# Five buffers for arriving weights in the MLP, taken from the up products' scratch, with the normed rows split by group and the loads of their sums moved ahead

## The chip, the core and the metric

The kernel runs on one core of one Trainium2 chip. The core has TensorE (PE in the profile; its weight loads are PEld), VectorE (DVE), ScalarE (ACT), GpSimd (POOL) and SyncE (SP), and 16 DMA engines that serve DMAs issued by SP, ACT and POOL. Each engine works through its own instructions in order. The metric is the device time in microseconds of one execution; lower is better.

## The reference, cut to what matters

```python
def encoder_layer(x, ...):
    h = rms_norm(x, g_mix)
    proj = h @ w_in                      # q, k, v, u/v of the gate, two gates
    attn = attention_mixer(q, k, v)      # 3 dilated windows, combined
    sgu = spatial_gating(u, vs, w_s, b_s, g_sgu)
    merged = sigmoid(ga) * (attn @ w_branch_a) + sigmoid(gb) * (sgu @ w_branch_b)
    x = x + merged @ w_out
    h2 = rms_norm(x, g_mlp)
    x = x + square(relu(h2 @ w_up)) @ w_down
    return x                             # then rms_norm(x, g_final)
```

There are 1536 tokens (512 of one request and 1024 of another), the width is 1024 and the MLP's inner width 4096; everything is float32. The change concerns the end of the `w_out` product, where `h2` is made, and the MLP.

## The kernel before, in words

**Split products.** A float32 matrix product is made of three passes of PE: each operand is split into a rounded part `hi` (a cast on ACT, line L153) and a rest `lo = src - hi` (a subtraction on DVE, L154), and `hi*hi`, `hi*lo` and `lo*hi` are added in PSUM.

**Weights.** `weight` (L157 to L164) brings one block of 512 x 128 or 128 x 512 weights: SP issues the load into a buffer `raw` (L159, 256 KB), ACT casts it to `hi`, DVE makes `lo`. There are N_RAW = 3 buffers `raw` and N_SPLIT = 5 pairs `hi`/`lo`, each used in turn. A load into a `raw` buffer waits until the split of the weight that was in it is done; a cast waits until PE has used the pair that it will overwrite.

**The w_out stage** (from about 1680 us to 1770 us). Two halves of columns times twelve tiles of 128 tokens. In the second half, each tile's finished row is stored (`x1_scr`, L819), normed (`h2`), transposed on PE (L744), multiplied by the gain on DVE (`h2T`, L746) and stored by SP to `h2_scr`, two stores of 512 x 128 per tile (L749).

**The MLP** (from 1774.75 us). The tokens form two groups of 768 (g = 0, 1). `h2` of a group, `w_up`, the activations and `w_down` are each cut into 2 x 2 blocks, and a product of two such matrices is made of seven products of blocks (`p1, p2, q3` to `q7`) instead of eight, by sums and differences of blocks. For each group there are eight steps c; a step has two up products (`up_products`, j = 0, 1: seven forms of 12 matmuls 128 x 384, L928) and one down product (`down_products`: seven forms of 18 matmuls 128 x 512, L979). Every form takes one weight in an up product and two in a down product, so 28 in a step. Below, U is the pair of up products of a step and D its down product.

In an up product DVE and ACT make the four blocks of activations out of the seven accumulators: `v` (L936), `z` (L943), `a22` (L946), `a21` (L951), `a12` (L956), then squares of their positive parts (ACT, L915 and L916) and the split forms for the down product. `q3` accumulates onto the bank of `q5`, which `a22` reads, and so its matmuls wait for `a22`. All these small results live in `unit` buffers of 128 x 384, twelve in turn.

**The forms of h2.** Each group starts from 28 blocks `hf` (seven forms times four k). `p1, p2, q4` are blocks of `h2` in `h2_scr`; `q3, q5, q6, q7` are sums of such blocks, made once on DVE and kept in `form_scr`. For group 0 the sums are made during the last tiles of the w_out stage: `diff_steps` gives a list of steps for each k (`loads`, then four sums, each with its store), all on POOL's queue, in rooms of rows that are already stored; `SUMS_AT` says how many steps follow each tile. For group 1 the same steps go along with group 0's steps c = 1 to 4 on SP's queue, in `unit` buffers. `form_steps` loads a block into a `unit` (`raw_form`, POOL's queue, L1026) and splits it (ACT, DVE); a load is issued N_FORM = 7 blocks ahead of the split. Group 0's forms enter in the first up product, group 1's in the last step of group 0, in its second up product and its down product.

**Other work.** Group 0's results are kept in `row_scr` and finished in group 1's steps 1 to 6 (`stored_steps`: loads of a row and of the gain on POOL's queue at L1061 and L240, a norm, a store). In a down product POOL makes three additions per tile (L995, L996, L1006).

**What sets the order.** A scheduler puts each engine's instructions in order from the program as written; `side()` hangs one step of the lists above behind each form of an up product and each tile of a down product.

Of the kernel before, what the change touches and what calls it, by code (L numbers as in the profile page):

```python
# [10 lines left out]
F32 = mybir.dt.float32  # L11
# [7 lines left out]
P = 128  # L19
DM = 1024  # L20
KB = DM // P
NTOK = 1536
# [10 lines left out]
BIG = 1e30  # L33
ROW = 2 * 64 + 4
EDGE = 24
N_SPLIT, N_RAW = 5, 3
QT = 2
STEPS = 49 / 36
XSTEP = 4
# [5 lines left out]
GT = NTOK // 2  # L45
HT = GT // 2
SUM_ROWS = 8
EARLY = 2
N_FORM = 7
SUMS_AT = {6: 1, 7: 5, 8: 5, 9: 5, 10: 4}  # L50
DIFFS = ("q3", "q5", "q6", "q7")
UP_ORDER = ("p1", "q6", "q7", "p2", "q5", "q4", "q3")
# [56 lines left out]
def encoder_kernel(ctx: ExitStack, tc: tile.TileContext, a):  # L109
    nc = tc.nc  # L110
# [8 lines left out]
    dram = ctx.enter_context(tc.tile_pool(name="dram", bufs=1, space=DRAM))  # L119
# [3 lines left out]
    wp = ctx.enter_context(tc.tile_pool(name="w", bufs=1))  # L123
# [11 lines left out]
    gate_scr = [dram.tile([P, NTOK], F32, name=f"gate_scr{m}") for m in range(EARLY)]  # L135
    form_scr = [dram.tile([len(DIFFS), 4, P, HT], F32, name=f"form_scr{g}") for g in range(2)]
    row_scr = dram.tile([GT, DM], F32, name="row_scr")
    h2_scr = dram.tile([KB, P, NTOK], F32, name="h2_scr")
    x1_scr = dram.tile([NTOK, DM], F32, name="x1_scr")
    up_sums = {k: dram.tile([DM // 2, DFF // 2], F32, name=f"up_{k}") for k in SUMS}  # L140
    down_sums = {k: dram.tile([DFF // 2, DM // 2], F32, name=f"down_{k}") for k in SUMS}
# [10 lines left out]
    def split(hi, lo, src, eng=nc.vector):  # L152
        nc.scalar.copy(hi, src)  # L153
        eng.tensor_sub(lo, src, hi.bitcast(F32))  # L154

    def weight(src, k, pair=None, eng=nc.vector):

        raw = wp.tile([P, 512], F32, tag="raw", name="raw", bufs=N_RAW).rearrange("p (k n) -> p k n", k=k)
        nc.sync.dma_start(out=raw, in_=src.rearrange("(k p) n -> p k n", p=P))  # L159
        if pair is None:  # L160
            pair = (wp.tile([P, 512], F32R, tag=s, name=s, bufs=N_SPLIT) for s in ("hi", "lo"))
        hi, lo = (t.rearrange("p (k n) -> p k n", k=k) for t in pair)
        split(hi, lo, raw, eng)
        return hi, lo  # L164
# [10 lines left out]
    def product_steps(out, terms):  # L175
        n = len(terms)
        for i, ((sh, sl), (mh, ml)) in enumerate(terms):
            nc.tensor.matmul(out, sh, mh, start=i == 0, stop=False)  # L178
            nc.tensor.matmul(out, sh, ml, start=False, stop=False)  # L179
            nc.tensor.matmul(out, sl, mh, start=False, stop=i == n - 1)  # L180
            yield
# [75 lines left out]
    with ExitStack() as ph:  # L257
# [6 lines left out]
        def load_x(t):  # L264
            raw = vpool.tile([P, 1024], F32, tag="x", name="x", bufs=2)
            parts = row_parts()
            for i in range(2):
                cols = slice(i * 512, (i + 1) * 512)
                eng = (nc.scalar, nc.sync)[i] if t == 0 else nc.gpsimd
                eng.dma_start(out=raw[:, cols], in_=x_rows[t][:, cols])  # L270
                if t == 0 and i:
                    junk = vpool.tile([P, 512], F32, tag="junk", name="junk", bufs=1)
                    nc.vector.tensor_tensor_reduce(
                        out=junk, in0=raw[:, cols], in1=raw[:, cols], scale=0.5 / DM, scalar=0.0,
                        op0=ALU.mult, op1=ALU.add, accum_out=parts[:, i:i + 1])
                else:
                    square_sum(parts[:, i:i + 1], raw[:, cols], vpool)
            rstd = rstd_of(parts)
            for i in range(2):
                cols = slice(i * 512, (i + 1) * 512)  # L280
                normed(raw[:, cols], raw[:, cols], rstd, g_mix[:, cols])
            return raw
# [4 lines left out]
        with ExitStack() as ph_w:  # L287
# [8 lines left out]
            for ch in range(2):  # L296
# [6 lines left out]
                for t in range(NT):  # L303
                    more_x = ch == 0 and t + 1 < NT
                    if more_x:
                        raw = load_x(t + 1)
                    acc = acc_tile()
                    steps = product_steps(acc, token_terms(hT[t // 4], t, lambda k: tuple(x[:, 0, :] for x in w[k])))
# [62 lines left out]
    with ExitStack() as ph:  # L371
# [230 lines left out]
        for c in range(SUM_ROWS):  # L602
            n = DM // 2 // SUM_ROWS
            streams.append(block_sums(a["w_up"][0], up_sums, DM // 2, DFF // 2, c * n, n))
            n = DFF // 2 // SUM_ROWS
# [41 lines left out]
    with ExitStack() as ph:  # L647
# [3 lines left out]
        def half_tile(name):  # L651
            return fp.tile([P, 512], F32, tag="half", name=name)
# [34 lines left out]
        for n in range(NCH):  # L687
            sig = {}
            attT = tuple(resident2(f"att_{s}") for s in "hl")
            for i in range(2 * KB):  # L690
                s, m = divmod(i, KB)
# [14 lines left out]
            for k in range(KB):  # L706
                raw = half_tile("sgu_raw")
# [31 lines left out]
    def h_features(t, halves):  # L739

        for i, h in enumerate(halves):
            pt = tp_tile()
            for b in range(4):
                nc.tensor.transpose(pt[:, b * P:(b + 1) * P], h[:, b * P:(b + 1) * P], ident)  # L744
            hT2 = pp.tile([P, 512], F32, tag="half", name="h2T", bufs=2)
            nc.vector.tensor_mul(  # L746
                hT2.rearrange("p (k t) -> p k t", k=4), pt.rearrange("p (k t) -> p k t", k=4),
                g_mlp[:, 4 * i:4 * i + 4, None].to_broadcast([P, 4, P]))
            nc.sync.dma_start(  # L749
                out=h2_scr[4 * i:4 * i + 4, :, t * P:(t + 1) * P].rearrange("k p t -> p k t"),  # L750
                in_=hT2.rearrange("p (k t) -> p k t", k=4))

    def diff_steps(g, k, new, eng, wait):

        x = {}

        def load(key, r, s):
            x[key] = new()
            eng.dma_start(out=x[key], in_=h2_scr[4 * s + k, :, g * GT + r * HT:g * GT + (r + 1) * HT])

        def store(form, key):
            eng.dma_start(out=form_scr[g][DIFFS.index(form), k], in_=x[key])

        def loads():
            load("a", 0, 0)
            load("b", 1, 0)
            load("c", 1, 1)
            load("d", 0, 1)

        def first():  # L770
            nc.vector.tensor_sub(x["a"], x["a"], x["b"])
            store("q7", "a")

        def second():
            nc.vector.tensor_sub(x["b"], x["b"], x["c"])
            store("q5", "b")

        def third():
            nc.vector.tensor_add(x["c"], x["a"], x["c"])
            store("q6", "c")  # L780

        def fourth():
            nc.vector.tensor_sub(x["d"], x["d"], x["c"])
            store("q3", "d")

        return [loads] + [lambda: None] * wait + [first, second, third, fourth]

    sums = []
    for k in range(4):

        room = [x1[(2 * k + i // 2) % 6][:, i % 2 * HT:(i % 2 + 1) * HT] for i in range(4)]
        sums += diff_steps(0, k, lambda room=room: room.pop(0), nc.gpsimd, 0)
    for ch in range(2):
        cols = slice(ch * 512, (ch + 1) * 512)
        w = {}
# [1 line left out]
        for k in (range(KB), (6, 7, 0, 1, 2, 3, 4, 5))[ch]:  # L797
            pair = None
            if len(w) >= (0, 2)[ch] and len(w) < (6, 8)[ch]:
                if not spare:  # L800
                    r = resident2("w_out")
# [4 lines left out]
        for t in range(NT):  # L806
            acc = acc_tile()
            terms = token_terms(hT[t // 4], t, lambda k: tuple(x[:, 0, :] for x in w[k]))
            steps = product_steps(acc, [terms[k] for k in w])
# [30 lines left out]
    mp = ctx.enter_context(tc.tile_pool(name="mlp", bufs=1, reuse_waits="tile"))  # L840
    slabs = ctx.enter_context(tc.tile_pool(name="slabs", bufs=6, side="right", reuse_waits="tile"))
    ps3 = ctx.enter_context(tc.tile_pool(name="ps3", bufs=8, space=PSUM, reuse_waits="tile"))
    def unit(name):
        return mp.tile([P, HT], F32, tag="unit", name=name, bufs=12)

    def bank():
        return ps3.tile([P, 512], F32, tag="acc", name="acc")
# [47 lines left out]
            self(len(self.steps))  # L895

    side = Side()

    def slab_view(s):
        return s.rearrange("p a b c -> p (a b c)").bitcast(F32)[:, :DM]  # L900
# [110 lines left out]
    def form_source(g, form, k):  # L1011
        if form in DIFFS:
            return form_scr[g][DIFFS.index(form), k]
        r, s = {"p1": (0, 0), "p2": (0, 1), "q4": (1, 1)}[form]
        return h2_scr[4 * s + k, :, g * GT + r * HT:g * GT + (r + 1) * HT]

    def form_steps(g, fs):

# [3 lines left out]
        def step(i):  # L1022
            for j in range(i, min(i + N_FORM, len(items))):
                if j not in raws:
# [71 lines left out]
    x = None  # L1096
    CH = DFF // P // 4
    for g in range(2):
        for c in range(CH):
# [5 lines left out]
            for j in range(2):  # L1105
# [5 lines left out]
                if not c and j:  # L1111
                    x = {}
# [49 lines left out]
```

## Time and profile before

| | us |
|---|---|
| median of 3 runs (lowest, highest) | 2806.36 (2803.49, 2807.26) |
| profiled execution, its own time | 2803.75 |
| its span | 2802.0 |
| PE busy | 2692.5 (96%) |
| DVE busy | 1747.7 (62%) |
| ACT busy | 1290.1 (46%) |
| POOL busy | 422.5 (15%) |
| granted TensorE clock, mean | 0.986 |

A table by stretches gives for each stretch `A:B` (us from the span's start) its length, the busy time of each engine with its instructions in brackets, the granted clock as a share of full speed, the mean busy share of the DMA engines and GB/s. A row of the waits reads: engine and line that waits, `<-` who ended the wait, then us in total, times, longest. A row of the timeline begins with its start and its length in us; in square brackets stands the idle time before it and who ended it. A row of the DMAs gives KB each and the us from issue to landing.

### The profile page before, as it was taken

Reading aid. Unit: us, or ns where it says so; the run is one execution under the profiler, and the core shown is the slowest. Engines: PE = TensorE matmul, PEld = TensorE weight load, DVE = VectorE, ACT = ScalarE, POOL = GpSimd, SP = SyncE. Lnnn points to the kernel's source line nnn. Section 1 sums busy time; section 2 is a strip of 40 time slices with the busy share of each in tenths; the row PEclk is TensorE's granted clock in tenths of the full one; section 3 lists DMA queues with packets and bytes.
Section 4 is the critical chain, followed back from the end, with each engine's and each line's share of the span. In section 5 each row is a group of like instructions: output and inputs, shape, how many; then the busy total and the mean of one; then the engine's idle time right before and its main releaser. Section 6 shows DMA issues by size and latency. Waiting matters only on the chain.

```text
span 2802.0 us, 38921 instructions
## 1 busy us (share of the span) xinstructions
PE 2692.5 (96%) x13400; PEld 2309.0 (82%) x13400; DVE 1747.7 (62%) x3722; ACT 1290.1 (46%) x2766; POOL 422.5 (15%) x507
## 2 busy tenths in 40 slices
PE   7999999999999999999999999899999989999997
PEld 5788888888888887888888887788989878888886
DVE  5542200166666666556555526788888868888888
ACT  5421111255556566553434321555556545555555
POOL 1000000011121212100000002222211322222222
PEclk9999999999999999999999999899999989999998
DMA  3112222247576768554443437654544555444443
GB/s 128 53 49 75 89 76 79 87 112 179 151 176 180 174 174 193 132 153 140 136 144 119 141 118 244 229 150 146 152 143 129 161 189 156 141 142 136 139 143 128
DMA packets 376439, 391.16 MB, mean 140 GB/s; under 512 B 23088, under 2 KB 290352, under 8 KB 372656
## 3 DMA queue, kind: packets, MB, share of 16 engines
q1 hardware_dynamic: 337008, 253.85, 30.3%
q0 software_dynamic: 28112, 86.83, 12.8%
q10 hardware_dynamic: 11120, 47.98, 5.0%
q8 instruction: 106, 1.74, 0.3%
q14 instruction: 93, 0.76, 0.1%
HBM read 333.22 MB, written 122.45 MB: 163 GB/s over the span
## 4 chain that ended last, share of the span: by engine, by line
PE 35%; DVE 8%; DMA 6%; issue 4%; ACT 4%; POOL 3%; DVEq 0%; SPq 0%; ACTq 0%; POOLq 0%
PE acc L979 7%; PE acc L178 7%; PE acc L180 7%; PE acc L179 7%; PE acc L928 6%; DVE lo L154 3%; DMA raw<-up_q 3%; ACT hi L153 1%; POOL x L996 1%; POOL x L995 1%; DVE act L154 1%; DMA raw<-in_w_down_dram 1%; ACT a L916 1%; ACT a L915 1%; ACT act L153 1%
## 5 line engine op out<-in xcount | busy, mean ns | idle before, releaser
L154 DVE TENSOR_TENSOR lo<-raw,hi 128x512 fp32r<-128x512 f32 x695 | 556.2, 805 | 420.8 <-ACT hi L153 413.8
L153 ACT CAST hi<-raw 128x512 fp32r<-128x512 f32 x696 | 430.6, 619 | 686.4 <-PE acc L179 238.3
L178 PE MATMUL acc<-res_h,hi 128*128 128x512 f32 x1344 | 556.2, 414 | 0.8 <-DVE stg L579 0.8
L180 PE MATMUL acc<-res_h,lo 128*128 128x512 f32 x1344 | 526.5, 392 | 0.0
L179 PE MATMUL acc<-res_l,hi 128*128 128x512 f32 x1344 | 525.3, 391 | 0.0
L928 PE MATMUL acc<-hf,hi 128*128 128x384 f32 x1792 | 471.6, 344 | 46.0 <-DVE a L946 24.8
L979 PE MATMUL acc<-hi,act 128*128 128x512 f32 x1344 | 423.9, 395 | 6.6 <-ACT hi L153 6.6
L928 PEld LDWEIGHTS acc<-hf,hi 128*128 128x128 f32 x1792 | 331.8, 193 | 59.2 <-ACT hi L153 30.8
L979 PEld LDWEIGHTS acc<-hi,act 128*128 128x128 f32 x1344 | 255.6, 191 | 61.4 <-ACT hi L153 8.9
L928 PE MATMUL acc<-hf,lo 128*128 128x384 f32 x896 | 306.1, 342 | 0.0
L180 PEld LDWEIGHTS acc<-res_h,lo 128*128 128x128 f32 x1344 | 252.4, 188 | 54.5
L179 PEld LDWEIGHTS acc<-res_l,hi 128*128 128x128 f32 x1344 | 254.3, 189 | 36.0
L178 PEld LDWEIGHTS acc<-res_h,hi 128*128 128x128 f32 x1344 | 254.0, 189 | 36.4 <-DVE stg L579 0.9
L979 PE MATMUL acc<-lo,act 128*128 128x512 f32 x672 | 266.1, 396 | 5.1 <-DVE lo L154 5.1
L551 ACT ACTIVATE pr<-pr,stg 128x128 f32<-128x128 f32 (+2 forms) x288 | 125.9, 438 | 175.8 <-DVE stg L548 139.5
L928 PEld LDWEIGHTS acc<-hf,lo 128*128 128x128 f32 x896 | 172.9, 193 | 0.9 <-DVE lo L154 0.8
L979 PEld LDWEIGHTS acc<-lo,act 128*128 128x128 f32 x672 | 128.3, 191 | 34.5 <-DVE lo L154 8.0
L521 DVE TENSOR_TENSOR q<-qT,q 64x256 fp32r<-64x256 f32 x288 | 120.7, 419 | 47.7 <-ACT q L518 43.9
L573 PEld LDWEIGHTS o<-v,pT 128*128 128x128 f32 x896 | 120.4, 191 | 24.9 <-DVE pT L563 14.7
L563 DVE COPY pT<-tp 128x512 f32<-128x512 f32 (+1 forms) x144 | 82.2, 571 | 93.9 <-PE tp L561 92.8
L995 POOL TENSOR_TENSOR x<-x,z 128x512 f32<-128x512 f32 x48 | 70.5, 1469 | 426.9 <-DVE z L994 426.8
L573 PE MATMUL o<-v,pT 128*128 128x64 f32 x896 | 117.3, 268 | 7.9 <-DVE pT L563 7.7
(186 smaller groups left out, 4119.9 us busy)
## 6 DMA issues: line engine op xcount, KB each, us to landing
raw<-in_w_in_dram SPq DMA_DIRECT2D x192, 256.0 KB, 3.0
raw<-up_q SPq DMA_DIRECT2D x128, 256.0 KB, 2.9
raw<-down_q SPq DMA_DIRECT2D x128, 256.0 KB, 2.7
raw<-in_w_up_dram SPq DMA_DIRECT2D x96, 256.0 KB, 2.9
raw<-in_w_down_dram SPq DMA_DIRECT2D x96, 256.0 KB, 2.9
up_q<-in_w_up_dram POOLq DMA_DIRECT2D x32, 512.0 KB, 9.3
down_q<-in_w_down_dram POOLq DMA_DIRECT2D x32, 512.0 KB, 10.9
raw<-in_w_branch_b_dram SPq DMA_DIRECT2D x48, 256.0 KB, 2.8
```

The source lines that it names most:

```text
L153: nc.scalar.copy(hi, src)
L154: eng.tensor_sub(lo, src, hi.bitcast(F32))
L178: nc.tensor.matmul(out, sh, mh, start=i == 0, stop=False)
L179: nc.tensor.matmul(out, sh, ml, start=False, stop=False)
L180: nc.tensor.matmul(out, sl, mh, start=False, stop=i == n - 1)
L521: nc.vector.tensor_sub(q2[rows, h, 1, :], src, q2[own, h, 0, :].bitcast(F32))
L551: last_of["act"] = nc.scalar.activation(pr[:, h, at:at + kn], pr[:, h, at:at + kn], AF.Exp, bias=low, scale=-1.0, accum_out=stg[:, j, 130 ...
L563: nc.vector.tensor_copy(self.pT[:, :n], pt[:, :n])
L573: nc.tensor.matmul(o[:, (2 * j + h) * 64:(2 * j + h + 1) * 64], self.pT[:, q * P:(q + 1) * P], found["v"][:, slot, h * 64:(h + 1) * 64], s ...
L928: nc.tensor.matmul(acc, st, mv, start=not on and k == 0 and n == 0, stop=k == 3 and n == 2, skip_group_check=bool(on))
L979: nc.tensor.matmul(acc, st, mv, start=not on and k == 0 and n == 0, stop=k == 1 and n == 2, skip_group_check=bool(on))
L995: nc.gpsimd.tensor_sub(x21, x21, z)
```

## The change

It has three parts. In the MLP a weight's `raw` buffer is taken in turn from five: three as before and two in the MLP's own pool, which exists only from the start of the MLP. Of every five weights, counted from the MLP's first, the third and the fourth take a new buffer. To make room, the `unit` buffers go from twelve to ten and N_FORM from 7 to 5. `h2_scr` becomes two tensors, one for each group. And the `loads` step of each k of group 0's sums is put four steps earlier in the list.

```diff
-N_SPLIT, N_RAW = 5, 3
+N_SPLIT, N_RAW, MORE_RAW = 5, 3, 2
...
-N_FORM = 7
+N_FORM = 5
...
-    h2_scr = dram.tile([KB, P, NTOK], F32, name="h2_scr")
+    h2_scr = [dram.tile([KB, P, GT], F32, name=f"h2_scr{g}") for g in range(2)]
...
+    more_raw = []
+
+    def raw_tile():
+
+        pool, bufs = wp, N_RAW
+        if more_raw:
+            at = more_raw[1] = (more_raw[1] + 1) % (N_RAW + MORE_RAW)
+            if at >= N_RAW:
+                pool, bufs = more_raw[0], MORE_RAW
+        return pool.tile([P, 512], F32, tag="raw", name="raw", bufs=bufs)
+
     def weight(src, k, pair=None, eng=nc.vector):
 
-        raw = wp.tile([P, 512], F32, tag="raw", name="raw", bufs=N_RAW).rearrange("p (k n) -> p k n", k=k)
+        raw = raw_tile().rearrange("p (k n) -> p k n", k=k)
...
-                out=h2_scr[4 * i:4 * i + 4, :, t * P:(t + 1) * P].rearrange("k p t -> p k t"),
+                out=h2_scr[t // 6][4 * i:4 * i + 4, :, t % 6 * P:(t % 6 + 1) * P].rearrange("k p t -> p k t"),
...
-            eng.dma_start(out=x[key], in_=h2_scr[4 * s + k, :, g * GT + r * HT:g * GT + (r + 1) * HT])
+            eng.dma_start(out=x[key], in_=h2_scr[g][4 * s + k, :, r * HT:(r + 1) * HT])
...
-        sums += diff_steps(0, k, lambda room=room: room.pop(0), nc.gpsimd, 0)
+        steps = diff_steps(0, k, lambda room=room: room.pop(0), nc.gpsimd, 0)
+
+        sums.insert(max(0, len(sums) - 4), steps[0])
+        sums += steps[1:]
...
-        return mp.tile([P, HT], F32, tag="unit", name=name, bufs=12)
+        return mp.tile([P, HT], F32, tag="unit", name=name, bufs=10)
...
     side = Side()
+    more_raw += [mp, 0]
...
-        return h2_scr[4 * s + k, :, g * GT + r * HT:g * GT + (r + 1) * HT]
+        return h2_scr[g][4 * s + k, :, r * HT:(r + 1) * HT]
```

Lines of the changed kernel lie 11 to 15 below those of before (the load of a weight at L170, a store of `h2T` at L760, a form's load at L1041).

The order of the instructions changes at three places that the prediction speaks of. The first is SP around the end of the w_out stage: weights of the first up product among the stores of rows and of `h2T`. Of before, the loads ahead of the stage's last stores, and those at its end (`up_q_102`, `101`, `100`, `103` are the blocks of q6, q7, q5, q4, `in_w_up_dram` those of p1, p2, q3):

```order
L159 DMA raw<-in_w_up_dram 128x4x128
L159 DMA raw<-up_q_102 128x4x128
L159 DMA raw<-up_q_101 128x4x128
L159 DMA raw<-in_w_up_dram 128x4x128
L159 DMA raw<-up_q_100 128x4x128
L819 DMA x_scr<-x_0_13923 128x1024
L159 DMA raw<-up_q_103 128x4x128
...
L159 DMA raw<-in_w_up_dram 128x4x128 x2
L819 DMA x_scr<-x_11_13956 128x1024
L749 DMA h_scr<-h2T 128x4x128 x4
L159 DMA raw<-up_q_102 128x4x128
```

The same places now (here `up_q_103`, `102`, `101`, `104` are q6, q7, q5, q4):

```order
L170 DMA raw<-in_w_up_dram 128x4x128
L170 DMA raw<-up_q_103 128x4x128
L170 DMA raw<-up_q_101 128x4x128
L170 DMA raw<-up_q_104 128x4x128
L170 DMA raw<-in_w_up_dram 128x4x128
L833 DMA x_scr<-x_0_13924 128x1024
...
L833 DMA x_scr<-x_11_13957 128x1024
L760 DMA h_scr_99<-h2T 128x4x128 x4
L170 DMA raw<-up_q_102 128x4x128
L170 DMA raw<-in_w_up_dram 128x4x128 x2
L170 DMA raw<-up_q_103 128x4x128
```

Before, p1, q6, q7, p2, q5 and q4 were loaded ahead and q3 and the next p1 before the last stores; now p1, q6, q5, q4 and q3 are loaded ahead, and q7 and p2 only behind the last store.

The second place is ACT at the MLP's start, the casts of forms (`hf`) and of weights (`hi`). Of before:

```order
L153 CAST hi<-raw 128x512 x2
L234 ACTIVATE junk,xp_13958<-x_11_13956 128x512
L153 CAST hf<-raw_form 128x384 x8
L933 COPY p_15219<-acc 128x384
L153 CAST hf<-raw_form 128x384 x2
L153 CAST hi<-raw 128x512 x2
L153 CAST hf<-raw_form 128x384 x4
```

And now:

```order
L245 ACTIVATE junk,xp_13956<-x_11_13957 128x512
L153 CAST hf<-raw_form 128x384
L153 CAST hi<-raw 128x512
L153 CAST hf<-raw_form 128x384 x2
L153 CAST hi<-raw 128x512
L153 CAST hf<-raw_form 128x384 x3
L153 CAST hi<-raw 128x512
L153 CAST hf<-raw_form 128x384
L948 COPY p_15216<-acc 128x384
L153 CAST hf<-raw_form 128x384
L153 CAST hi<-raw 128x512 x2
```

Two casts of weights ahead of the last tile's squares are gone from there, and three stand between the first eight casts of forms. At the switch of groups ACT's casts of weights likewise stand earlier and more evenly among those of the forms; in group 1's steps 1 to 6 the orders on ACT and DVE are as before.

The third place is POOL in the w_out stage, where group 0's sums are loaded and stored. Of before:

```order
L762 DMA form_scr_95<-x_3_13932 128x384 x2
L759 DMA x_0_13923<-h_scr 128x384 x2
L762 DMA form_scr_95<-x_4_13935 128x384
L759 DMA x_1_13926<-h_scr 128x384 x2
L762 DMA form_scr_95<-x_4_13935 128x384
```

And now:

```order
L773 DMA form_scr_95<-x_3_13933 128x384 x2
L770 DMA x_0_13924<-h_scr_98 128x384 x2
L770 DMA x_1_13927<-h_scr_98 128x384 x2
L773 DMA form_scr_95<-x_4_13936 128x384 x2
L773 DMA form_scr_95<-x_5_13939 128x384
```

The loads into `x_1` now stand ahead of one store instead of behind it; the other loads and stores of these sums keep their places.

## The prediction

> **What bounds the kernel now.** First the page: its engine line says who is busy, the groups what PE waits for.
>
> ```profile
> span 2802.0 us, 38921 instructions
> PE 2692.5 (96%) x13400; PEld 2309.0 (82%) x13400; DVE 1747.7 (62%) x3722; ACT 1290.1 (46%) x2766; POOL 422.5 (15%) x507
> ...
> L928 PE MATMUL acc<-hf,hi 128*128 128x384 f32 x1792 | 471.6, 344 | 46.0 <-DVE a L946 24.8
> ```
>
> PE is the bound over the whole; what is left is its idle time and the slow clock behind each idle stretch. The up products (L928) hold 46.0 us of idle, more than half of it waiting for DVE's a22 (L946). So the next view is the table by stretches, cut where PE passes between up products (U below, a pair of 14 weights) and down products (D).
>
> ```profile
> core 0: us, PE busy (x) PEld busy (x) DVE busy (x) ACT busy (x) POOL busy (x), PEclk, DMA share, GB/s
> 1774.75:1814.61 39.86, 36.12 (x170) 32.52 (x171) 34.18 (x67) 30.78 (x66) 10.31 (x20) 0.90 0.76 258
> 1842.76:2140.99 298.23, 291.25 (x1471) 263.74 (x1470) 249.46 (x408) 166.40 (x316) 70.44 (x45) 1.00 0.49 146
> 2020.76:2052.89 32.13, 29.72 (x169) 29.10 (x168) 24.96 (x41) 20.51 (x40) 4.69 (x3) 1.00 0.46 132
> 2140.99:2170.44 29.45, 29.45 (x169) 29.12 (x168) 24.20 (x40) 20.13 (x40) 4.68 (x3) 1.00 0.48 139
> 2170.44:2199.04 28.60, 28.60 (x127) 23.67 (x127) 22.88 (x37) 12.65 (x24) 8.89 (x6) 1.00 0.38 107
> 2228.01:2279.21 51.20, 39.59 (x142) 29.77 (x141) 41.32 (x70) 25.38 (x55) 22.74 (x30) 0.87 0.52 168
> 2279.21:2313.20 33.99, 31.02 (x168) 30.11 (x166) 22.39 (x39) 18.94 (x38) 4.23 (x5) 0.95 0.70 228
> 2313.20:2344.25 31.05, 29.33 (x126) 23.44 (x127) 27.83 (x41) 13.54 (x25) 10.18 (x8) 1.00 0.55 155
> 2344.25:2725.43 381.18, 359.66 (x1766) 326.25 (x1764) 325.20 (x537) 205.27 (x403) 93.55 (x88) 0.97 0.49 141
> 2725.43:2755.06 29.63, 29.44 (x170) 29.12 (x168) 24.33 (x40) 20.53 (x40) 5.25 (x4) 1.00 0.48 140
> 2755.06:2787.67 32.61, 30.93 (x127) 24.52 (x126) 28.08 (x51) 15.71 (x37) 14.20 (x9) 0.95 0.26 84
> ```
>
> The first row is the first U of the MLP; an undisturbed U takes 29.45 and a D 28.60 (rows 4 and 5). Row 2 is group 0's steps 1 to 5, five U and five D: (298.23 - 5 x 28.60) / 5 = 31.05 for a U, the worst 32.13 (row 3). Row 6 is the D that ends group 0, while group 1's rows are split: 51.20. Rows 7 and 8 are group 1's step 0, row 9 its steps 1 to 6, six U and six D: the six U take 381.18 - 6 x 28.60 = 209.6, 34.9 each. Row 10 is step 7's U, row 11 the last D.
>
> The waits of row 9's stretch (counted from 2330 to 2700), and inside it one U, that of step 3, from the timeline:
>
> ```profile
> PE acc L928 <- DVE a L946: 18.2, 6, 3.5
> ACT hi L153 <- DMA raw<-up_q: 48.7, 17, 5.7
> ...
> 2464.94 3.35 DVE L154 TENSOR_TENSOR lo<-raw,hi 128x512 fp32r<-128x512 f32 x1
> 2465.18 1.30 POOL L995 TENSOR_TENSOR x<-x,z 128x512 f32<-128x512 f32 x1
> 2473.02 0.62 ACT L153 CAST hi<-raw 128x512 fp32r<-128x512 f32 x1 [5.04 <-DMA raw<-up_q]
> 2478.72 0.62 ACT L153 CAST hi<-raw 128x512 fp32r<-128x512 f32 x1 [3.58 <-DMA raw<-up_q]
> 2487.60 0.55 DVE L946 TENSOR_TENSOR a<-z,acc 128x384 f32<-128x384 f32 x1
> 2488.29 0.59 PE L928 MATMUL acc<-hf,hi 128*128 128x384 f32 x2 [1.99 <-DVE a L946]
> 2490.17 0.84 PE L928 MATMUL acc<-hf,hi 128*128 128x384 f32 x2
> ```
>
> One split on DVE takes 3.35 us beside POOL's adds; its raw buffer comes free late, and SP's next load into it waits for that; ACT waits 5.04 and 3.58 for landed weights, and the splits that stand ahead of a22 on DVE are late. PE then waits 1.99 (3.5 at worst) for a22, since q3 accumulates onto the bank that a22 reads, and works at a lower pace behind the wait: two matmuls take 0.84 at 2490.17 where two took 0.59.
>
> **The change part by part.**
>
> *Five raw buffers, group 1 steps 1 to 6.* ACT's and DVE's order is unchanged there; only loads start earlier, at the split of five weights ago instead of three. PE uses one weight of a U per 29.45 / 14 = 2.1 us, so two more buffers are 4.2 us of head start, more than the 3.5 of the worst wait. If so, a22 is no longer late, and the clock stays. The six U then lie between the 31.05 of group 0 and step 7's 29.63: I take 30.5, a gain of 209.6 - 183.0 = 26.6. Ends: all six at 32.13 gives 16.8, all at 29.63 gives 31.8.
>
> What speaks against it is how long a load takes with more of them in flight:
>
> ```profile
> raw<-up_q SPq DMA_DIRECT2D x51, 256.0 KB, 3.0
> ...
> raw<-up_q SPq DMA_DIRECT2D x4, 256.0 KB, 4.5
> ```
>
> The first row is from 2330 to 2725, the second from 1770 to 1800, where the engines were fullest. The bytes are the same and the share in row 9 of the table is 0.49, so I keep 3.0. The Trainium skill, DMA: Bandwidth & Descriptors, "Issuing engines are not separate DMA queues", says that all DMAs run on the same 16 engines and interleave. If five loads in flight shared them evenly, as an estimate by that page each would land in 3.0 x 5 / 3 = 5.0, the head start would shrink from 4.2 to 2.2, and this term would be its lower end, 16.8, with the sum some 10 smaller. The trace so far shows 4.5 only where forms are loaded as well.
>
> *The switch of groups (rows 6 to 8).*
>
> ```profile
> ACT hi L153 <- DMA raw<-in_w_down_dram: 14.5, 4, 6.9
> PE acc L979 <- DVE lo L154: 4.9, 4, 2.0
> POOL raw_form L1026 <- DVE hf L154: 8.5, 5, 2.7
> ```
>
> ACT waits 14.5 for weights in that D, and the new order has its casts of weights earlier among those of the forms. But DVE is busy for 41.32 of the 51.20 and most of it must be done before the D ends: the floor is about 41.3, and I take 42.5, a gain of 8.7. The U behind it comes to group 0's 31.05 (2.9), the D after it loses its wait for a cast (1.5 of 31.05 - 28.60). Together 13.1. Ends: 9.9 + 4.5 + 2.4 = 16.8; and 0, if POOL, which already waits 8.5 for units to come free, waits 8.5 x 12 / 10 = 10.2 with ten units instead of twelve, the D grows by these 1.7, and the U only comes down to 32.13.
>
> *Group 0.*
>
> ```profile
> PE acc L928 <- DVE a L946: 3.4, 4, 1.7
> ```
>
> From 1840 to 2200 this is all that the change can take; I take 2.5. On SP the loads of the differences and the stores of sums move one pair of weights later, in four steps; a store waits for DVE's difference, and the weights queued behind it wait too. I cost that at nothing, since the two more buffers are full by then. With that cover gone, four U at the worst length instead of the mean lose 4 x (32.13 - 31.05) = 4.3. Ends: -4.3 and 3.4.
>
> *The last D* waits for a cast, and goes from 32.61 towards 28.60; its end is tied to the rows' finishing, so 1.5 (0 to 4.0).
>
> *The first U (row 1).* This is where something is given up. Before, p1, q6, q7, p2, q5 were loaded and split long ahead, and q4 and q3 loaded; now two of the five buffers exist only once the MLP's pool opens, so q7 and p2 are loaded behind the last store of rows and three splits (q7, p2, q5) stand between those of the forms.
>
> ```profile
> 1770.00:1780.00 10.00, 5.25 (x16) 4.95 (x17) 4.19 (x8) 4.77 (x10) 8.30 (x16) 0.51 0.94 301
> 1780.00:1800.00 20.00, 18.53 (x98) 16.42 (x97) 18.77 (x38) 17.44 (x39) 6.61 (x13) 1.00 0.69 218
> ...
> 1780.47 0.62 ACT L153 CAST hi<-raw 128x512 fp32r<-128x512 f32 x1
> 1781.14 0.68 DVE L154 TENSOR_TENSOR lo<-raw,hi 128x512 fp32r<-128x512 f32 x1
> PE acc L928 <- ACT hi L153: 2.3, 1, 2.3
> ```
>
> DVE has 18.77 of 20 us to do there, ACT 17.44, so three more splits are 3 x 0.68 = 2.0 on the path; and ACT, which works in order, will hold a form behind a cast whose weight lands in the fullest 10 us (share 0.94): about 1.5. Against it the 2.3 that the second half of this U now waits for a cast should go, as its weights come earlier. Net +1.2 (from -2.3 to +6).
>
> *Split tensors and moved loads.* Each group's loads already waited only for stores into their own part, so two tensors change no wait. Of the moved loads one pair now passes one store on POOL's queue:
>
> ```profile
> 1739.69 1.06 POOL L759 DMA_DIRECT2D x<-h_scr  x2
> 1740.74 1.08 POOL L762 DMA_DIRECT2D form_scr<-x  x2
> ```
>
> A store's issue takes 0.54, and DVE's sums there wait for these loads: gain 0.3 (0 to 0.8; the transposes behind wait for an earlier load that is not moved).
>
> **Sum**: 26.6 + 13.1 + 2.5 + 1.5 - 1.2 + 0.3 = 42.8. The profiled execution took 2803.75, so 2761; it lay 2.6 under the median shown, so I give 2762 for a median.
>
> **The rivals.**
>
> *DVE, not the raws.* The splits that POOL's adds stretch stay as long. If they themselves, not the late loads, make a22 late, row 9 keeps its length. For it: 325.20 of 381.18 is 85% DVE. Against it: the 3.35 split ended at 2468.3, 19 us ahead of the late a22, and DVE's idle time between is spent on casts that wait for loads. Then only half of the switch (6), the last D and the 0.3 stay: 2803.75 - 6 - 1.5 - 0.3 + 1.2 = 2797. The Trainium skill, SBUF — State Buffer, "Who interferes with whom", states that a DVE instruction with two SBUF inputs and a GpSimd one that reads SBUF block each other for a whole instruction; by that rule the stretch outlives any number of buffers. The trace agrees that such a split is stretched, though 3.35 is longer than one add.
>
> *More in flight, all later (the slower side).* Forms and weights share one set of engines. The landing of a form, and the first and the last of the 28 casts of forms at the MLP's start:
>
> ```profile
> DMA to landing us min/median/max: 2.6/4.1/5.6
> ...
> 1774.18 2.13 ACT L153 CAST hf<-raw_form 128x384 fp32r<-128x384 f32 x4 [9.24 <-DMA raw_form<-h_scr]
> 1795.57 0.50 ACT L153 CAST hf<-raw_form 128x384 fp32r<-128x384 f32 x1
> ```
>
> Two further weights in flight can push everything back. A raw buffer is held for a cast and a stretched split, 0.62 + 3.35 = 4.0, beside its landing: with three, a weight comes every (4.0 + 3.0) / 3 = 2.3, slower than PE's 2.1, and five give nothing once (4.0 + L) / 5 = 2.3, at L = 7.7. Forms that land in 7.7, ten in flight, come every (0.54 + 7.7 + 0.5 + 0.55) / 10 = 0.93 (issue, landing, cast, split), where they now take 21.9 / 28 = 0.78: over the 56 forms of both groups 8 us are lost, and the time is 2812. It decides from a landing of 7.7; the longest median seen is 4.5, the longest form 5.6.
>
> *The raws do half.* With the stretched splits as they are, five buffers bridge some of the six waits and not all: 13 instead of 26.6, 2776.
>
> **How the numbers follow.** My forecast 0.66; half 0.14; DVE 0.12; more in flight 0.08. The upper ends add to 31.8 + 16.8 + 3.4 + 4.0 + 2.3 + 0.8 = 59, 2745 at best; the lower ends, 16.8 + 0 - 4.3 - 6, come to 6.5, 2797. The range, 2745 to 2798, holds these and the DVE case; the slower one and what lies past the ends stay out. About 0.2% (5.6 us) is what a measurement here tells from no change: faster 0.66 + 0.14 + half of 0.12 = 0.86, same 0.06, slower 0.08.
>
> **What the new profile would show.** Right: the wait of L928's PE rows for a22 falls from 18.2 to under 6, the clock of group 1's steps 1 to 6 is 1.00 instead of 0.97, casts wait for up_q there under 15 us instead of 48.7; six U of 30 to 31; the D at the switch 41 to 44; the first U 38 to 45. Wrong: ACT's waits for up_q gone but a22 as late (DVE); landings of raw over 5 (more in flight); a first U of 50 and more, or PE waiting for forms at the switch, which would mean that the units were dear. I would be wrong by most if the switch, where DVE sets the floor, gave nothing.

## The result, and the profile after

The changed kernel takes 2759.53 us in the median (2756.71 to 2764.94, 4 runs), the kernel before 2805.82 beside it (2803.49 to 2807.26): a ratio of 0.9838, with a 95% interval from 0.9821 to 0.9855. The profiled execution took 2760.84, its span is 2759.0. The prediction was 2762 and "faster". The sum came out by luck: three of its terms were off by 5.5 to 8.5 us, and these errors nearly cancelled.

The page of the changed kernel, engine line and the group of the up products (L943 is L928 of before, L994 is L979, L961 is L946):

```profile
PE 2676.8 (97%) x13400; PEld 2294.2 (83%) x13400; DVE 1745.5 (63%) x3722; ACT 1289.9 (47%) x2766; POOL 422.9 (15%) x507
...
L943 PE MATMUL acc<-hf,hi 128*128 128x384 f32 x1792 | 463.2, 338 | 13.2 <-ACT hf L153 8.6
```

The idle time ahead of these matmuls falls from 46.0 us to 13.2, and the wait for a22 has left the first place: what remains is the wait for the first forms. The same stretches as in the prediction, cut at the same products:

```profile
1775.38:1816.97 41.59, 37.70 (x178) 33.04 (x178) 33.99 (x66) 32.13 (x70) 10.33 (x20) 0.91 0.83 267
1845.08:2135.29 290.21, 290.19 (x1472) 263.83 (x1470) 249.32 (x407) 165.96 (x316) 71.34 (x45) 1.00 0.49 149
2222.76:2269.13 46.37, 35.83 (x132) 26.01 (x131) 36.30 (x61) 22.48 (x48) 21.82 (x29) 0.93 0.58 183
2269.13:2303.50 34.37, 30.93 (x166) 29.74 (x164) 24.04 (x40) 18.54 (x38) 4.50 (x6) 0.95 0.73 229
2303.50:2334.36 30.86, 29.13 (x126) 23.60 (x127) 27.65 (x42) 14.49 (x27) 9.64 (x8) 1.00 0.52 156
2334.36:2682.74 348.38, 348.36 (x1765) 316.36 (x1764) 322.97 (x536) 204.87 (x403) 93.81 (x88) 1.00 0.53 154
2712.18:2743.19 31.01, 29.35 (x127) 23.38 (x126) 26.48 (x49) 15.33 (x36) 14.19 (x9) 1.00 0.21 68
```

Rows 2 and 6 are the reading of this case. In group 0's steps 1 to 5 and group 1's steps 1 to 6 PE is busy for the whole length (290.19 of 290.21, 348.36 of 348.38), at full clock: each U takes (348.38 - 6 x 28.60) / 6 = 29.5. DVE did the same work in row 6 as before (322.97 us against 325.20) in 33 us less, so it was never the bound there, only kept waiting. The stretched split is still there, and ACT hardly waits for loads:

```profile
2443.52 3.35 DVE L154 TENSOR_TENSOR lo<-raw,hi 128x512 fp32r<-128x512 f32 x1
...
ACT hi L153 <- PE acc L994: 76.3, 32, 2.8
ACT hi L153 <- DMA raw<-up_q: 6.7, 6, 1.4
```

The first line is step 3's split, 3.35 us long as in the kernel before; the other two are ACT's waits from 2330 to 2700. The wait for up_q was 48.7 and is 6.7, and casts now wait for PE to free a pair, so weights stand ready ahead of PE.

Where the 43.0 us of the span went, stretch by stretch (before, after, difference, and what the prediction had):

| stretch | before | after | difference | predicted |
|---|---|---|---|---|
| up to the MLP's start | 1774.75 | 1775.38 | +0.6 | -0.3 |
| first U and its D | 68.01 | 69.70 | +1.7 | +1.2 |
| group 0, steps 1 to 5 | 298.23 | 290.21 | -8.0 | -2.5 |
| group 0, step 6 and U of step 7 | 87.02 | 87.47 | +0.5 | 0 |
| switch: D, U, D | 116.24 | 111.60 | -4.6 | -13.1 |
| group 1, steps 1 to 6 | 381.18 | 348.38 | -32.8 | -26.6 |
| from group 1's step 7 to the end | 76.57 | 76.26 | -0.3 | -1.5 |

The rows of a single trace scatter: the changed kernel's second profile has 68.88 us for the first U and its D and 113.44 for the switch. Of the prediction's own signs, the wait for a22, the casts' wait for up_q, the clock and the first U came as said; the six U of 30 to 31 (29.5 now) and the D of 41 to 44 at the switch (46.37) did not.

### The profile page after: what moved, and what is told of

Same layout as the page of the kernel before. It is cut to its first block, busy times and chain, and to the rows that moved or that the text cites. A ratio compares the mean times of both kernels' runs of the same rounds, so it can differ in the third digit from the quotient of the medians.

```text
span 2759.0 us, 38938 instructions
## 1 busy us (share of the span) xinstructions
PE 2676.8 (97%) x13400; PEld 2294.2 (83%) x13400; DVE 1745.5 (63%) x3722; ACT 1289.9 (47%) x2766; POOL 422.9 (15%) x507
## 4 chain that ended last, share of the span: by engine, by line
PE 54%; DVE 2%; DMA 1%; issue 1%; ACT 1%; POOL 0%; SPq 0%; DVEq 0%; POOLq 0%; ACTq 0%
PE acc L943 17%; PE acc L994 15%; PE acc L189 7%; PE acc L191 7%; PE acc L190 7%; DMA raw<-up_q 0%; DVE lo L154 0%; PE o L584 0%; PE tp L755 0%; PE s L545 0%; DVE x L248 0%; DMA x<-h_scr 0%; POOL raw_form L1041 0%; PE tp L259 0%; DMA form_scr<-x 0%
## 5 line engine op out<-in xcount | busy, mean ns | idle before, releaser
L943 PE MATMUL acc<-hf,hi 128*128 128x384 f32 x1792 | 463.2, 338 | 13.2 <-ACT hf L153 8.6
L994 PE MATMUL acc<-hi,act 128*128 128x512 f32 x1344 | 421.3, 392 | 5.0 <-ACT hi L153 3.4
L943 PEld LDWEIGHTS acc<-hf,hi 128*128 128x128 f32 x1792 | 325.2, 189 | 24.8 <-ACT hf L153 10.3
L943 PE MATMUL acc<-hf,lo 128*128 128x384 f32 x896 | 301.1, 337 | 2.9 <-DVE lo L154 2.9
L994 PEld LDWEIGHTS acc<-hi,act 128*128 128x128 f32 x1344 | 253.4, 189 | 60.0 <-ACT hi L153 6.0
L994 PE MATMUL acc<-lo,act 128*128 128x512 f32 x672 | 264.2, 393 | 7.5 <-DVE lo L154 7.3
L943 PEld LDWEIGHTS acc<-hf,lo 128*128 128x128 f32 x896 | 169.6, 189 | 3.2 <-DVE lo L154 3.2
L994 PEld LDWEIGHTS acc<-lo,act 128*128 128x128 f32 x672 | 127.0, 189 | 36.8 <-DVE lo L154 10.7
```

What stands on the lines that cost most here:

```text
L943: nc.tensor.matmul(acc, st, mv, start=not on and k == 0 and n == 0, stop=k == 3 and n == 2, skip_group_check=bool(on))
L994: nc.tensor.matmul(acc, st, mv, start=not on and k == 0 and n == 0, stop=k == 1 and n == 2, skip_group_check=bool(on))
```

## The experiments

The theory: loads wait for raw buffers that a late split holds; two more buffers bridge that. The rivals: DVE's stretched splits themselves set the pace; or another part of the change carries the gain.

### Each part alone

The three parts were taken apart: five raws with ten units and a look-ahead of five, nothing else of the change; the split tensors and the moved loads alone; and ten units with a look-ahead of five alone.

```diff
 raws_only (against the kernel before)
-N_SPLIT, N_RAW = 5, 3
+N_SPLIT, N_RAW, MORE_RAW = 5, 3, 2      # and raw_tile(), as in the change
-N_FORM = 7
+N_FORM = 5
-... tag="unit", name=name, bufs=12)
+... tag="unit", name=name, bufs=10)

 tensors_only (against the changed kernel)
-N_SPLIT, N_RAW, MORE_RAW = 5, 3, 2
+N_SPLIT, N_RAW, MORE_RAW = 5, 3, 0
-    more_raw += [mp, 0]
-N_FORM = 5
+N_FORM = 7
-... bufs=10)
+... bufs=12)

 units_only (against the kernel before)
-N_FORM = 7
+N_FORM = 5
-... bufs=12)
+... bufs=10)
```

Expected of raws_only:

> The kernel before with five raw buffers, ten units and a look-ahead of five forms; h2_scr stays one tensor and the loads of sums stay where they were. If the raws carry the change: 2759 within 4, and the six U of group 1's steps 1 to 6 at 29.5 each as in the changed kernel. If the split tensors or the moved loads carry a part: more than 2764.

Of tensors_only:

> The changed kernel with three raw buffers, twelve units and a look-ahead of seven again, so only the split h2_scr and the moved loads are left. By the prediction's 0.3 us: 2805 within 4, the MLP starting at the same time within 0.8. If these two parts matter: below 2799.

Of units_only:

> The kernel before with ten units and a look-ahead of five, and still three raws: the price of what was given up, alone. If units were spare: 2806 within 3. If the forms starve without them, as the slower end of the prediction's terms had it: the first U grows by 2 to 6 and the D at the switch by about 2, 2809 to 2814.

Measured: raws_only 2759.61 (ratio 0.9826, 0.9810 to 0.9843), tensors_only 2809.73 (1.0001, 0.9991 to 1.0011), units_only 2808.54 (0.9998, 0.9988 to 1.0007), where the kernel before took 2809.61. The stretches of group 1's steps 1 to 6, in this order:

```profile
2331.83:2680.34 348.51, 348.49 (x1766) 316.48 (x1764) 322.99 (x536) 204.84 (x403) 93.62 (x88) 1.00 0.53 154
```

```profile
2347.91:2731.11 383.20, 358.32 (x1765) 324.26 (x1764) 325.02 (x537) 205.15 (x403) 93.50 (x88) 0.97 0.48 140
```

```profile
1777.74:1815.10 37.36, 33.94 (x168) 30.29 (x169) 30.77 (x61) 29.09 (x63) 10.29 (x20) 0.95 0.74 236
1815.10:1847.72 32.62, 30.89 (x127) 24.59 (x127) 23.84 (x40) 14.15 (x26) 9.29 (x6) 0.95 0.50 155
...
2346.34:2729.21 382.87, 360.33 (x1766) 326.12 (x1764) 324.55 (x537) 205.19 (x403) 93.52 (x88) 0.97 0.48 140
```

The raws carry the gain as a whole. Splitting the tensor and moving the loads gives nothing that can be measured: tensors_only lies on the kernel before, though above the 2805 within 4 that was expected, as does the kernel before itself on this chip, and its MLP starts 3.0 us later instead of within 0.8, as that of units_only does. Giving up two units and two forms of look-ahead costs nothing as a whole, but moves time about. The last fence's first two rows are units_only's first U and its D: together 69.98, nearly the changed kernel's 69.70, but made up otherwise. With three raws the U takes 37.36 and the D, where PE waits 2.2 us for casts of weights, 32.62; with five raws the U takes 41.59 and the D 28.11; before, they took 39.86 and 28.15. So the fewer units and the shorter look-ahead alone don't lengthen the U; with the five raws beside them it is longer, and the D shorter.

### Four buffers

```diff
-N_SPLIT, N_RAW, MORE_RAW = 5, 3, 2
+N_SPLIT, N_RAW, MORE_RAW = 5, 3, 1
```

> The changed kernel with one new raw buffer instead of two. If a buffer is worth 2.1 us of head start, four of them bridge the waits of 2.0 us and leave up to 1.4 of the 3.5 in each of group 1's steps 1 to 6: these steps take about 355 us (381 with three buffers, 348 with five), the whole about 2768. If the fourth buffer already does all: 2760. If there is a threshold that only five pass: 2790 and more.

Measured: 2770.88 (0.9863, 0.9845 to 0.9882). Group 1's steps 1 to 6 and PE's waits in them:

```profile
2336.23:2694.02 357.79, 350.01 (x1765) 316.18 (x1764) 321.52 (x536) 204.83 (x403) 93.63 (x88) 1.00 0.51 150
```

```profile
PE acc L943 <- ACT p L948: 4.3, 6, 0.7
PE acc L943 <- DVE a L961: 3.5, 6, 1.2
```

Buffers count as head start: one more takes 23 of the 33 us, the second the other 9, within 3 us of the expected 355 and 2768. The longest wait for a22 is 1.2, where 3.5 - 2.1 = 1.4 was expected. More than half of the waiting that is left is for p1's copy on ACT, which the expectation did not count; in these steps ACT's casts still wait for loads, up to 4.7 us for one.

### What makes the raws late

```diff
 no_stored_rows (against the kernel before, three raws)
-            if g and 1 <= c <= 6:
-                side.add(stored_steps(c - 1))
```

> The kernel before, three raws, without the finishing of group 0's rows in group 1's steps 1 to 6 (loads of rows and of the gain on POOL's queue, norm, store; 768 of the 1536 rows are not written). If POOL's loads between its additions are what stretches the splits and so keeps the raws: the six U come down from 34.9 to group 0's 31.0, steps 1 to 6 from 381 to about 358, the whole to about 2783. If the additions alone do it: steps 1 to 6 stay above 375, the whole above 2798.

Measured, one run: 2777.76. Group 1's steps 1 to 6, and their splits (duration min, median, max in ns):

```profile
2349.94:2699.53 349.59, 348.26 (x1765) 316.65 (x1764) 292.85 (x469) 199.16 (x378) 81.55 (x54) 1.00 0.44 127
```

```profile
L154 DVE TENSOR_TENSOR lo<-raw,hi x168: 674/691/1780, 2351.0 to 2698.5; 128x512 fp32r<-128x512 f32 x168
```

With three buffers, but without the finishing of rows, the steps take 349.59, nearly the 348.38 of five buffers, more of a gain than the 358 that was expected. The longest split is 1.78 us instead of 3.36, though POOL's additions are still made. So the late raws of group 1 come with the stored rows; in group 0's steps 1 to 5, which have POOL's additions but no stored rows, the longest split of the kernel before is 1.78 us as well. By the timeline their DMAs on POOL's queue stand between POOL's additions and the stretched splits beside them; DVE's row norms are extra work too. Both were left out together, so this run doesn't divide the loss between them.

### What holds the switch

```diff
 no_form_rests (against the changed kernel; put() makes only the cast of group 1's forms)
-            fs[k].put(form, raws[i])
+            fs[k].put(form, raws[i], not g)
```

> The changed kernel without DVE's 28 subtractions for group 1's forms (PE takes the rests of group 0's forms that still lie there): 28 x 0.55 = 15 us less on DVE from 2200 to 2270. If DVE's work is what keeps the switch long: its D falls from 46.4 to 30 to 35 and the U behind it from 34.4 to about 31, the whole to 2745 within 5. If late weights or the casts on ACT keep it long: D stays above 43, the whole above 2754.

Measured, one run: 2746.25. The D, the U and the next D at the switch:

```profile
2225.11:2256.58 31.47, 29.97 (x128) 23.39 (x127) 25.00 (x40) 21.79 (x48) 20.26 (x28) 1.00 0.78 253
2256.58:2286.76 30.18, 29.61 (x169) 28.97 (x167) 23.31 (x39) 18.27 (x38) 5.62 (x6) 1.00 0.87 276
2286.76:2319.18 32.42, 30.68 (x127) 24.75 (x127) 27.68 (x42) 14.50 (x27) 9.65 (x8) 0.95 0.51 149
```

With DVE's 28 subtractions gone and as many loads, casts and buffers as in the changed kernel, the D falls from 46.37 to 31.47 and the U from 34.37 to 30.18. DVE's work on the forms is what makes the switch long. It need not act on PE alone: without the subtractions splits end earlier, so raws come free earlier too, and units come free at the cast. Whether more raws would also shorten the switch was not run. The next D gets no shorter (32.42; 30.86 and, in the second profile, 32.44 in the changed kernel): PE waits 1.7 us there for a cast that stands late in ACT's order.

### The price of the first up product

```diff
 new_raws_late
-    more_raw += [mp, 0]
+    more_raw += [mp, 4]

 forms_seven, forms_four
-N_FORM = 5
+N_FORM = 7        # and 4
```

> The changed kernel with the count of the raws begun so that the MLP's first three weights take the three old buffers and the fourth and fifth (p2, q5) the new ones: q7 is then loaded and split ahead of the MLP. If the late weights are what makes the first U long: 41.6 (to the D's first wait) falls by about 2, 2757. If the forms' casts set its pace: no change, 2759 within 2.

> The changed kernel with a look-ahead of seven forms again, with its ten units. If the units, not the look-ahead, set when a form is loaded: 2759 within 2.5. If the shorter look-ahead is what made the first U 1.7 us longer: 2756 to 2757 and a first U below 40.

> The changed kernel with a look-ahead of four forms instead of five. The units alone made the first U and its D 2.0 us longer, and a look-ahead of seven in ten units 4.2 us longer: if loads far ahead take units from the products' own results, four give back part of it, 1 to 2 us below the changed kernel, with first U and D at 68 to 69. If they are then too late: 1 to 4 us above it.

Measured: new_raws_late 2761.08 (0.9829, 0.9816 to 0.9842), forms_seven 2767.32 (0.9845, 0.9832 to 0.9859), forms_four 2762.58 (0.9832, 0.9814 to 0.9851). The first U and its D, in this order (forms_seven in two rows, the others in one):

```profile
1775.43:1845.98 70.55, 64.44 (x294) 54.63 (x295) 58.28 (x104) 44.09 (x91) 19.20 (x26) 0.94 0.69 220
```

```profile
1774.93:1814.64 39.71, 35.47 (x169) 30.25 (x169) 32.24 (x64) 30.28 (x66) 10.30 (x20) 0.93 0.79 253
1814.64:1847.09 32.45, 30.72 (x127) 24.75 (x127) 26.49 (x43) 14.49 (x27) 8.90 (x6) 0.95 0.52 164
```

```profile
1775.33:1847.54 72.21, 66.68 (x294) 55.78 (x295) 59.41 (x105) 44.83 (x92) 19.27 (x26) 0.92 0.68 217
```

Loading q7 early gives nothing (70.55 where the changed kernel has 69.70). But it doesn't free the U of late weights: now p2 is the late one, and ACT holds the forms for it, longer than for q7 in the changed kernel. The first line is from the changed kernel, the second from new_raws_late:

```profile
1776.71 0.62 ACT L153 CAST hi<-raw 128x512 fp32r<-128x512 f32 x1 [1.39 <-DMA raw<-up_q]
1777.71 0.62 ACT L153 CAST hi<-raw 128x512 fp32r<-128x512 f32 x1 [2.34 <-DMA raw<-in_w_up_dram]
```

Both other look-aheads take 2.5 us more for U and D. With seven, the U is below 40 as the second case had it (39.71), but the D behind it takes 32.45 instead of 28.11, and the whole, 2767.32, lies above both cases. With four it came as the second case said, 1.2 above the changed kernel on the same chip. How the look-ahead acts is not settled; all three ratios overlap that of the changed kernel.

### A version that is faster still

The changed kernel was run again beside these: 2761.37 (0.9827, 0.9811 to 0.9844).

> The changed kernel once more, beside the three that follow on the same chip: a ratio of 0.983 to 0.985 to the kernel before, 2762 where the kernel before takes 2809.

```diff
 pool_rests (put() passes eng on to split())
-            fs[k].put(form, raws[i])
+            fs[k].put(form, raws[i], nc.gpsimd if g and i >= 20 else nc.vector)
```

> The changed kernel with the subtractions of group 1's last eight forms (q4, q3) on POOL instead of DVE. If DVE's work sets the switch and POOL has room: 8 x 0.67 = 5 us less on DVE, the D 3 to 5 shorter than 46.4, the whole 3 to 5 below the changed kernel run beside it. If POOL's subtractions block DVE's, or put POOL's additions in the D later: the same or up to 4 above.

> Both together. If they act at different places (the first U and the switch) their gains add: 4 to 7 us below the changed kernel. If the look-ahead is also what POOL's subtractions need at the switch: no better than the better of the two.

Measured: pool_rests 2754.76 (0.9807, 0.9790 to 0.9825), with a look-ahead of four 2759.01 (0.9821, 0.9803 to 0.9840). The switch in pool_rests:

```profile
2222.70:2267.54 44.84, 33.19 (x127) 24.96 (x127) 42.60 (x56) 22.34 (x48) 31.02 (x37) 0.89 0.57 180
2267.54:2297.95 30.41, 29.61 (x170) 28.97 (x168) 20.62 (x36) 18.28 (x38) 4.70 (x6) 1.00 0.85 272
2297.95:2328.76 30.81, 29.09 (x126) 23.60 (x127) 27.63 (x42) 14.49 (x27) 9.63 (x8) 1.00 0.51 154
```

The gain is 6.6 us against the changed kernel on the same chip. Each run of pool_rests (2754.04 to 2758.80) lies below each of the changed kernel (2760.01 to 2762.86), though the intervals of the two ratios overlap. It isn't where it was expected: the D is 44.84, only 1.5 shorter, with DVE busier than before (42.60), and the U behind it gains 4.0: it no longer waits for a split. Why the U gains and the D does not was not followed up. The two edits together give no more than one.

## Why the prediction was right, and where its steps were not

**Five raws in group 1.** The mechanism was right: the wait for a22 went from 18.2 to none that the view lists, the clock to 1.00, with ACT's and DVE's order as it was. The term was mis-sized: 26.6 predicted, 32.8 measured, past even its upper end of 31.8. The step that failed is the choice of 30.5 for a U, taken between two measured lengths without naming a wait that would keep it above the undisturbed 29.45. One that could was PE's wait on p1's copy, which comes after casts on ACT; but ACT was late because those casts waited for loads. With four buffers these waits are there still (4.3 in six), with five they are gone, and the U takes 29.5.

**Group 0.** A short wait was passed over again, at more cost: 3.4 was called all that the change can take, from the one row on a22. The measured 8.0 is those 3.4, the 3.6 that PE waited for p1's copy in the same stretch,

```profile
PE acc L928 <- ACT p L933: 3.6, 5, 0.7
```

and about 1 us behind the waits. A wait on ACT's copy should have been followed back to what ACT had waited for. The moved diff loads on SP cost nothing, as predicted.

**The switch.** 13.1 predicted, 4.6 measured. The floor was the failing step: 41.3 us of DVE work was taken as the D's floor with 1.2 us to spare. It was no floor, as some of that work can stand elsewhere (DVE has 61 instructions in the D now instead of 70, and the same 162.15 us from group 0's step 6 to group 1's step 0); and it was no estimate, for the D came to 46.37 with DVE busy for 36.30 of it. DVE's work there comes in chains with ACT, PE and late loads. PE's two longest waits in the D, 3.96 and 2.90 us, both lead back to a cast that waited for its weight:

```profile
2234.23 0.62 ACT L153 CAST hi<-raw 128x512 fp32r<-128x512 f32 x1 [2.88 <-DMA raw<-down_q]
2235.29 1.03 DVE L154 TENSOR_TENSOR hf<-raw_form,hf 128x384 fp32r<-128x384 f32 x2 [2.83 <-ACT hf L153]
2236.97 0.68 PE L994 MATMUL acc<-lo,act 128*128 128x512 f32 x1 [3.96 <-DVE lo L154]
...
2250.90 3.20 DVE L154 TENSOR_TENSOR hf<-raw_form,hf 128x384 fp32r<-128x384 f32 x2
2256.28 1.28 DVE L154 TENSOR_TENSOR lo<-raw,hi 128x512 fp32r<-128x512 f32 x2
2256.99 0.97 SPq L170 DMA_DIRECT2D raw<-up_q  x2
2262.97 0.62 ACT L153 CAST hi<-raw 128x512 fp32r<-128x512 f32 x1 [8.39 <-DMA raw<-up_q]
2263.65 0.61 PE L943 MATMUL acc<-hf,hi 128*128 128x384 f32 x2 [2.90 <-ACT hi L153]
2273.51 0.44 PE L943 MATMUL acc<-hf,lo 128*128 128x384 f32 x1 [2.89 <-DVE lo L154]
```

In the first chain the form's cast stands behind the late weight's on ACT, its subtraction waits for it, and the split that PE needs stands behind that on DVE. In the second, the load at 2256.99 goes out when a split has freed its buffer. The last line is the U behind the D, whose predicted gain of 2.9 was none: its wait of 2.78 for a22 became one of 2.89 for a split. That DVE's work on the forms makes the switch long is shown by no_form_rests; that the U and the next D would recover by themselves was only assumed.

Nor do the raws alone make the 4.6. The cut between U and D lies differently in the two traces (PE runs 142 matmuls in the one D, 132 in the other), so this is counted from group 0's step 6 to the end of group 1's step 0, for the kernel before, units_only, forms_seven and the changed kernel:

```profile
2140.99:2344.25 203.26, 185.63 (x883) 163.12 (x882) 162.15 (x261) 109.11 (x216) 60.25 (x63) 0.96 0.55 167
2144.68:2346.34 201.66, 186.75 (x884) 163.19 (x883) 162.76 (x261) 108.85 (x216) 59.46 (x63) 0.96 0.55 169
2137.33:2341.42 204.09, 187.02 (x883) 164.51 (x882) 165.72 (x262) 109.90 (x218) 58.10 (x63) 0.95 0.55 168
2135.29:2334.36 199.07, 183.35 (x883) 161.22 (x882) 162.15 (x262) 109.82 (x218) 59.11 (x63) 0.97 0.56 172
```

With ten units, five raws and a look-ahead of seven gain nothing here, three raws and a look-ahead of five gain 1.6, and five raws with five 4.2. So a part of the gain goes with the shorter look-ahead, which had no term in the prediction; only the fewer units had one, a possible loss of 1.7. That is one trace each, and the changed kernel's second profile has 200.93, so how this gain divides stays open.

**The last D.** 1.5 predicted, nothing gained at the end. The D itself is 1.6 shorter (31.01), but PE is idle for 1.7 us of it in both traces; what differs is the clock (0.95, now 1.00), and from its start to the end of the run there are 46.94 us before and 46.82 now. PE still waits 1.43 for a cast. Before, the view puts ACT's longest wait for a weight in this D at 3.4; now that is gone, and the cast stands behind the squares of the final rows in ACT's order:

```profile
2738.23 0.19 ACT L245 ACTIVATION_READ_ACCUMULATOR junk<-x 128x1 f32 x1
2738.32 0.60 ACT L153 CAST hi<-raw 128x512 fp32r<-128x512 f32 x1
2738.97 0.50 PE L994 MATMUL acc<-hi,act 128*128 128x512 f32 x1 [1.43 <-ACT hi L153]
```

**The first U.** 1.2 lost predicted, 1.7 measured in these two traces; the changed kernel's second profile has 68.88 us for U and D, so about 1 of it can be scatter. The mechanism is there: three casts of weights stand between the first casts of forms, ACT holds forms for 1.39 and 0.16 us where about 1.5 was predicted, and from the first cast of a form to p1's copy 6.73 us pass instead of 5.09. The 2.3 that PE waited for a cast in this U is gone, as predicted. But forms_seven, with the same 6.73 us, has a U of 39.71, so what follows on them counts too, and the cause of the 1.7 stays open.

**Split tensors and moved loads.** Nothing, within what can be told; the MLP starts between 1772.9 and 1778.8 us in the profiled executions of these kernels, so 0.3 us can't be seen.

**The rivals.** "DVE, not the raws" fell: 3.35 us splits and 323 us of DVE work are as before, and PE doesn't wait. "The raws do half" fell too: their term came out above its upper end. "More in flight, all later": from 2330 to 2690 up_q lands in 3.7 instead of 3.0, and the other weights as before (2.7 to 3.2; 2.7 to 3.3 before), far from the 7.7 from which this rival decides:

```profile
raw<-up_q SPq DMA_DIRECT2D x53, 256.0 KB, 3.7
```

So the even sharing that the rule of the Trainium skill (DMA: Bandwidth & Descriptors, "Issuing engines are not separate DMA queues") was taken to mean, 5.0 per load, was not seen. Nor was it put to the test: 168 weights in 348.38 us are one in 2.07 us, so at landings of 2.7 to 3.7 there were only 1.3 to 1.8 loads in flight on average, not five. That one kind of load lands later cost PE nothing.

## What to carry to other kernels

Where one late step holds a buffer, and the buffer the next load, look at the longest wait of the engine that bounds the kernel, divide by its time per buffer, and add that many buffers: here 3.5 us at 2.1 per weight, so two, and four_raws shows that one was not enough. Before taking a short wait as given, follow it one engine further back: the waits for DVE's a22 and for ACT's copy went together once loads came in time. The busy time of DVE in a stretch is neither a floor for it, where instructions can move to the next stretch, nor an estimate, where they come in chains. And two variants with the same sum over two stretches can differ in both: compare each.

## What the runs showed of the hardware that was not expected

A DVE subtraction with both inputs in SBUF can be held through several POOL instructions in a row. In pool_rests, on DVE and then on POOL:

```profile
2244.88 6.86 DVE L154 TENSOR_TENSOR hf<-raw_form,hf 128x384 fp32r<-128x384 f32 x1
...
2244.47 1.02 POOL L154 TENSOR_TENSOR hf<-raw_form,hf 128x384 fp32r<-128x384 f32 x1
2245.41 0.55 POOL L1041 DMA_DIRECT2D raw_form<-form_scr  x1
2245.99 1.95 POOL L154 TENSOR_TENSOR hf<-raw_form,hf 128x384 fp32r<-128x384 f32 x2
2247.89 1.27 POOL L1010 TENSOR_TENSOR x<-x,z 128x512 f32<-128x512 f32 x1
2249.11 1.26 POOL L1011 TENSOR_TENSOR x<-x,z 128x512 f32<-128x512 f32 x1
2250.33 0.98 POOL L154 TENSOR_TENSOR hf<-raw_form,hf 128x384 fp32r<-128x384 f32 x1
```

The subtraction, 0.55 us when alone, starts under the first of these and ends at 2251.74, 0.43 after the last one ends at 2251.31. The 3.35 us splits look the same on a smaller scale: the one shown ahead of the result, at 2464.94, begins under a DMA issue on POOL, ahead of the addition at 2465.18, and ends at 2468.29, behind that one and the next (to 2467.72). The Trainium skill, SBUF — State Buffer, "Who interferes with whom", has two such instructions block each other for a whole instruction; here DVE did not get its turn between POOL's instructions while these followed without a gap. That is read from the trace, not tested by a run of its own.
